# Neighbouring PSUM banks for pairs, with re-searched product tables, in a two-layer matmul kernel

## The chip, the cores and the metric

The kernel runs on one core of one Trainium2 chip. The metric is the device time of one launch in microseconds (us). The kernel before took 941.87 us (median of 3 runs, 941.43 to 942.97).

## The reference

```python
y = np.matmul(x, w1) + b1        # x (16, 512, 768), w1 (768, 3072)
y = np.maximum(y, 0)
return np.matmul(y, w2)          # w2 (3072, 768), all float32
```

In flat form, 8192 rows of x go through a first product (768 to 3072), bias and relu, and a second product (3072 to 768).

## The kernel before, in words

**Fewer products.** Both products are done by a recursive scheme of the Strassen kind in float16. Tables at the top of the file describe it. A first product of 3 x 2 blocks takes 20 block products instead of 24 (`FIRST_U`, `FIRST_V`), on sums of x blocks (`X_SUMS`) and of w1 blocks (`W1_SUMS`); a second product likewise takes 20 (`SECOND_U`, `SECOND_V`, `Y_SUMS`, `W2_SUMS`). `FIRST_OPS` and `SECOND_OPS` list what is done with the finished products in PSUM: write an output ('out'), keep a sum in SBUF ('sum'), or put the value in the PSUM of another chain as its start ('seed'). `FIRST_CHAINS` and `SECOND_CHAINS` say which products (m) and operations (t) follow each other in one piece of PSUM, and `FIRST_ORDER` and `SECOND_ORDER` give the order in which TensorE takes the products.

**Iterations.** There are 16, numbered 0 to 15: 8 blocks of 1024 rows for the first half of the hidden width, then 8 for the second half. Iteration 0 computes its first product plainly, without the scheme (L821). Each other iteration has two stages on TensorE: 40 first products of 6 matmuls each (L911, 256 columns), and 20 second products of 8 matmuls each (L1032, 384 columns). During the first stage ScalarE (ACT) and VectorE (DVE) evict into y (L941, L945, L948, L951, L957). During the second stage they work on pairs of banks (L1044 on ACT, L1047 on DVE), DVE adds y blocks (L884) and x blocks of the next iteration (L661), SyncE (SP) issues transposing DMAs into x (L612), and stores go out from SP or, with accumulation in DRAM, from GpSimd (POOL) (L1075, L1077). In the last iteration POOL adds sums to earlier results (L1085).

**PSUM.** The tile `ps` has 8 banks of 512 float32 on 128 partitions. A first product fills one bank. A second product needs two banks, for rows j = 0 and j = 1, and the eviction of both is one instruction over a view with the stride between the two banks. That view is `pair` (L1022 to L1024):

```python
        def pair(reg):
            a, b = reg.at
            return self.ps[:, a:b + 1:b - a, 0:NH]
```

**The order of the work.** Class `Graph` is a planner. Each piece of work is added with an engine and a written-in duration; `run` places the pieces in time on the five queues, and in `take` (L297 to L318) picks the banks for each piece of PSUM, by when they come free. In before, a pair is any two banks that come free first. The instructions are then issued in the planned order, each engine working strictly through its own queue. Semaphore waits are not written by hand: the layer that records the instructions adds them, from the regions of the tiles that each one reads and writes.

**Fused sums.** Two sums that follow each other in `X_SUMS` or `Y_SUMS` can be done by one DVE instruction over a strided view; `X_FUSE` and `Y_FUSE` name where.

Of the kernel before, what the change touches and what calls it, by code (L numbers as in the profile page):

```python
# [27 lines left out]

X_SUMS = ((20, 7, 5, -1), (18, 3, 2, -1), (13, 0, 6, -1), (8, 4, 5, -1), (22, 6, 7, -1), (21, 7,
    1, -1), (23, 4, 6, -1), (11, 2, 5, -1), (10, 3, 1, -1), (19, 4, 2, -1), (15, 2, 1, -1), (9, 6,
    5, -1), (12, 2, 0, -1), (17, 6, 1, -1), (16, 1, 0, -1), (14, 3, 5, -1))
FIRST_U = (8, 9, 21, 18, 2, 13, 20, 19, 1, 14, 10, 17, 11, 22, 6, 12, 5, 23, 15, 16)
W1_SUMS = ((6, 2, 5, 1), (8, 6, 4, -1), (17, 1, 8, -1), (7, 0, 1, 1), (10, 8, 7, -1), (16, 3, 10,
    -1), (9, 6, 3, -1), (11, 5, 4, -1), (12, 9, 0, -1), (14, 7, 9, -1), (15, 3, 5, -1), (13, 7, 2,
    -1))
FIRST_V = (2, 9, 4, 11, 17, 1, 3, 1, 16, 4, 3, 14, 8, 15, 12, 0, 6, 0, 10, 13)
FIRST_OPS = {
    0: (2, 1, 15, 1, 'out', 0, None),  # L40
    1: (3, 1, None, None, 'out', 1, (1.0, 1.0, -1.0)),
    2: (3, 1, 15, 1, 'out', 2, None),
    3: (0, 1, None, None, 'out', 3, None),
    4: (7, 1, 17, 1, 'out', 4, None),
    5: (7, 1, 19, 1, 'out', 5, None),
    6: (5, 1, 18, 1, 'out', 6, None),
    7: (4, 1, 17, 1, 'out', 7, None),
    8: (1, 1, 19, 1, 'out', 8, None),
    9: (6, 1, 18, 1, 'out', 9, None),
    10: (2, 1, None, None, 'out', 10, (0.0, 1.0, 0.0)),  # L50
    11: (6, 1, None, None, 'out', 11, (0.0, 0.0, 1.0)),
    12: (7, 1, None, None, 'seed', 4, None),
    13: (2, 1, None, None, 'seed', 3, (-1.0, 0.0, 1.0)),
    14: (6, 1, None, None, 'seed', 5, None),
    15: (8, -1, None, None, 'sum', None, (1.0, 0.0, 0.0)),
    16: (8, -1, 20, 1, 'seed', 0, None),
    17: (8, 1, 19, 1, 'sum', None, (0.0, 1.0, -1.0)),
    18: (2, -1, 20, 1, 'sum', None, None),
    19: (6, 1, None, None, 'sum', None, (0.0, 0.0, 1.0)),
    20: (2, 1, None, None, 'sum', None, (1.0, 0.0, 0.0)),  # L60
}
FIRST_CHAINS = ((('m', 10), ('t', 3)), (('m', 0), ('t', 8)), (('m', 8), ('t', 20), ('t', 0), ('m',
# [4 lines left out]
FIRST_SEEDS = (16, None, None, 13, 12, 14, None, None, None)  # L67
FIRST_ORDER = (36, 4, 16, 20, 12, 0, 8, 7, 9, 18, 24, 28, 10, 1, 15, 3, 21, 38, 32, 14, 35, 29,
    27, 30, 11, 34, 23, 26, 37, 31, 6, 5, 17, 25, 2, 22, 13, 33, 39, 19)
SWITCH_ORDER = (36, 4, 16, 20, 12, 0, 8, 7, 9, 18, 24, 28, 10, 1, 15, 3, 21, 38, 32, 14, 35, 29,  # L70
    27, 30, 11, 34, 23, 26, 37, 31, 6, 5, 17, 25, 2, 22, 13, 33, 39, 19)

Y_SUMS = ((16, 3, 0, 1), (21, 5, 3, 1), (15, 8, 7, 1), (12, 11, 10, 1), (19, 5, 16, 1), (18, 1,
    15, 1), (20, 2, 19, 1), (14, 6, 9, -1), (17, 11, 14, -1), (22, 1, 17, 1), (26, 18, 20, 1),
    (24, 7, 22, 1), (13, 4, 12, -1), (23, 11, 9, 1), (27, 13, 14, 1), (25, 13, 16, -1))
SECOND_U = (6, 2, 8, 26, 5, 21, 17, 23, 27, 19, 13, 4, 25, 12, 15, 11, 24, 18, 0, 1)
W2_SUMS = ((9, 2, 0, -1), (11, 9, 5, -1), (7, 2, 1, -1), (15, 5, 7, -1), (6, 5, 4, 1), (8, 6, 3,
    -1), (14, 8, 9, -1), (13, 3, 11, 1), (10, 7, 8, -1), (16, 10, 0, -1), (12, 7, 6, -1), (17, 5,
    2, -1))
SECOND_V = (0, 5, 7, 17, 9, 0, 10, 3, 16, 11, 14, 1, 13, 4, 1, 8, 12, 15, 3, 4)  # L80
W2_NEG = (4,)
SECOND_OPS = {
    0: (0, 1, 11, 1, 'out', 4, None),
    1: (2, 1, 9, 1, 'out', 5, None),
    2: (1, 1, 11, 1, 'out', 6, None),
    3: (2, 1, None, None, 'out', 7, None),
    4: (1, 1, 8, 1, 'out', 2, None),
    5: (3, -1, 8, 1, 'out', 3, None),
    6: (0, -1, 9, 1, 'out', 0, None),
    7: (3, 1, None, None, 'out', 1, None),  # L90
    8: (1, -1, 13, 1, 'sum', None, None),
    9: (0, 1, 10, 1, 'sum', None, None),
    10: (4, 1, 16, -1, 'sum', None, None),
    11: (5, 1, None, None, 'sum', None, None),
    12: (5, -1, None, None, 'seed', 0, None),
    13: (6, 1, None, None, 'sum', None, None),
    14: (5, 1, 16, 1, 'seed', 2, None),
    15: (1, -1, None, None, 'seed', 5, None),
    16: (1, 1, None, None, 'sum', None, None),
    17: (3, -1, 19, 1, 'seed', 1, None),  # L100
    18: (4, -1, None, None, 'seed', 3, None),
    19: (6, 1, None, None, 'sum', None, None),
# [6 lines left out]
SECOND_SEEDS = (12, 17, 14, 18, None, 15, None)  # L109
SECOND_ORDER = (19, 5, 1, 4, 9, 17, 13, 18, 15, 10, 12, 6, 7, 11, 2, 0, 14, 8, 16, 3)  # L110
LAST_ORDER = (19, 5, 1, 4, 9, 17, 13, 18, 15, 10, 12, 6, 7, 11, 2, 0, 14, 8, 16, 3)

X_FUSE = (3, 8, 11)
Y_FUSE = (2, 13)


def general_path(ctx, tc, xf, w1, b1, w2, of):
# [113 lines left out]
class Graph:  # L231
# [57 lines left out]
    def held(self, reg, at):  # L289
# [3 lines left out]
            self.places[reg.kind][i][0] = 1e9  # L293
        return reg

    def take(self, reg, start):

        p = self.places[reg.kind]
        if reg.kind == "ps":
            if reg.seeded:  # L300
                found = sorted((max(f, start), -full, i) for i, (f, full) in enumerate(p)
                               if full >= (2 if reg.seeded == 2 else 1))
            else:
                found = sorted((max(f, start), full, i) for i, (f, full) in enumerate(p))
            if len(found) < reg.n or found[reg.n - 1][0] > 1e8:
                return None
            at = sorted(i for _, _, i in found[:reg.n])
            return found[reg.n - 1][0], at
        best = None
        step = reg.n if reg.kind == "s" else 1  # L310
        for i in range(0, len(p) - reg.n + 1, step):
            f = max(p[k][0] for k in range(i, i + reg.n))
            if f < 1e8 and (best is None or f < best[0]):
                best = (f, list(range(i, i + reg.n)))
        return best
# [134 lines left out]
class Fast:  # L450
# [442 lines left out]
    def add_first(self, it):  # L893
# [12 lines left out]
        def product(p, ch, start):  # L906
            at = bank[ch].at[0]
            gi, p = divmod(p, np)
            for j in range(2):
                for k in range(3):  # L910
                    nc.tensor.matmul(  # L911
                        self.ps[:, at, j * self.QM:(j + 1) * self.QM],
                        lhsT=self.v1[:, gi, self.w1s[FIRST_V[p]], k, j * P:(j + 1) * P],
                        rhs=self.x[:, self.xs[FIRST_U[p]], k, :],
                        start=(start and j == 0 and k == 0), stop=(k == 2),
# [46 lines left out]
        for kind, n in sequence(chains, seeds, ops, SWITCH_ORDER if switch else FIRST_ORDER):  # L962
            if kind == "m":
# [46 lines left out]
    def add_second(self, it):  # L1010
# [7 lines left out]
        NH, QM = self.NH, self.QM  # L1018
# [1 line left out]
        last = [n for k, n in steps if k == "t" and SECOND_OPS[n][4] == "out"][-1]  # L1020

        def pair(reg):  # L1022
            a, b = reg.at
            return self.ps[:, a:b + 1:b - a, 0:NH]  # L1024

        def product(p, ch, start):
            sj = [(s, j) for s in range(4) for j in range(2)]
# [61 lines left out]
        for kind, n in steps:  # L1089
            if kind == "m":  # L1090
                ch = where[n]
                start = ch not in bank
# [8 lines left out]
            ch, a, u, b, what, to, _ = SECOND_OPS[n]  # L1101
# [231 lines left out]
```

## Time and profile before

| what | value |
|---|---|
| median of 3 runs | 941.87 us |
| the profiled execution | 942.75 us, span 941.1 us |
| granted TensorE clock, mean | 0.998 |
| busy over the span: PE, DVE, ACT, POOL | 865.2, 690.3, 477.8, 142.9 us |
| DMA queues, share of 16 engines | 42.0% (software), 25.5% (hardware) |

The profile is of one execution. Its page gives busy time by engine, the chain of work that ended last, and groups of equal instructions. "PE" is the matmul part of TensorE; "idle before" is the time the engine stood still just ahead of an instruction, with the instruction that released it. The busy time of PE counts overlapping matmuls once, so what it leaves of the span is idle time. The profile names tiles but not banks; the banks of an instruction and the semaphore counts that it waits for stand in the built program.

### The profile page before, as it was taken

The page shows a single profiled execution, that of the slowest core. Times are in us where ns is not written, and L with a number is a line of the kernel's source. Part 1 is how long each engine was busy: PE and PEld are TensorE (multiplying, and loading weights), DVE is VectorE, ACT ScalarE, POOL GpSimd, SP SyncE. Part 2 cuts the span into 40 slices and gives each one's busy share as a digit, 9 for nine tenths or more (in the row PEclk, how much of TensorE's full clock was granted, in tenths as well). Part 3 has the DMA queues.
Part 4 walks back from the last instruction along what each step waited for, and adds up shares of the span by engine and source line. Part 5 has one row for each costly group of instructions (what it writes and reads, how often), then busy time and mean ns, then how long its engine had stood idle before and what let it go on. Part 6 is the DMA issues. An engine that isn't in the chain of part 4 may idle for free.

```text
span 941.1 us, 16251 instructions
## 1 busy us (share of the span) xinstructions
PE 865.2 (92%) x6445; PEld 631.1 (67%) x6445; DVE 690.3 (73%) x1052; ACT 477.8 (51%) x951; POOL 142.9 (15%) x155
## 2 busy tenths in 40 slices
PE   8998989799897988989989999999989999899996
PEld 7567558486584855848668685866848576585763
DVE  3788768667686676776889879676867868668673
ACT  6866647366473662633745253744728325253340
POOL 5113100101001010000030402213030130401204
PEclk9999999999999999999999999999999999999999
DMA  9999583836638347361697958688686677943743
GB/s 211 193 220 194 95 198 68 159 101 87 175 68 160 99 77 185 69 134 68 223 200 115 134 85 133 112 116 128 102 116 104 103 117 102 144 75 51 104 133 135
DMA packets 162979, 119.86 MB, mean 127 GB/s; under 512 B 93244, under 2 KB 161364, under 8 KB 162644
## 3 DMA queue, kind: packets, MB, share of 16 engines
q0 software_dynamic: 49760, 58.99, 42.0%
q1 hardware_dynamic: 112672, 58.81, 25.5%
q8 instruction: 51, 0.84, 0.4%
q10 hardware_dynamic: 468, 1.00, 0.3%
q14 instruction: 28, 0.23, 0.1%
HBM read 73.94 MB, written 59.77 MB: 142 GB/s over the span
## 4 chain that ended last, share of the span: by engine, by line
PE 73%; DVE 10%; DMA 6%; issue 4%; ACT 4%; POOL 1%; SPq 0%; DVEq 0%; POOLq 0%; ACTq 0%
PE ps L911 39%; PE ps L1032 31%; DVE o L1047 3%; PE ps L821 3%; DVE y L884 3%; DMA x<-xn 2%; DVE s L1047 2%; DMA out_dram<-o 2%; ACT ps L1044 2%; DVE x L661 1%; DMA out_dram<-s 1%; ACT o L1044 1%; DMA v<-in_w_dram 1%; ACT xn L620 1%; DVE ps L1047 1%
## 5 line engine op out<-in xcount | busy, mean ns | idle before, releaser
L1032 PE MATMUL ps<-v,y 128*128 128x384 f16 x2560 | 430.9, 326 | 56.6 <-ACT ps L1044 18.9
L911 PE MATMUL ps<-x,v 128*128 128x256 f16 x3600 | 398.6, 273 | 9.4 <-DVE o L1047 2.6
L1032 PEld LDWEIGHTS <-y 128*128 128x128 f16 x2560 | 249.7, 98 | 233.6 <-issue 74.1
L911 PEld LDWEIGHTS <-v 128*128 128x128 f16 x3600 | 352.5, 98 | 54.6 <-issue 10.1
L948 DVE CUSTOM_DVE_ANT_0 y<-ps,s 128x512 f16<-128x512 f32 x240 | 157.6, 687 | 79.2 <-PE ps L911 75.3
L884 DVE TENSOR_TENSOR y<-y 128x1024 f16<-128x1024 f16 (+2 forms) x242 | 170.2, 718 | 8.5 <-ACT y L830 5.2
L945 ACT ACTIVATE s<-ps,bt 128x256 f32<-128x256 f32 x180 | 75.3, 469 | 141.1 <-PE ps L911 122.0
L661 DVE TENSOR_TENSOR x<-x 128x768 f16<-128x768 f16 (+1 forms) x182 | 112.8, 644 | 15.3 <-DMA x<-xn 14.3
L1077 POOL DMA_DIRECT2D out_dram<-o x68 | 81.6, 1282 | 213.9 <-DMA out_dram<-s 74.3
L1044 ACT ACTIVATE ps<-ps 128x768 f32<-128x768 f32 x48 | 38.2, 795 | 147.3 <-PE ps L1032 105.9
L558 POOL DMA_DIRECT2D xn<-in_x_dram x30 | 22.7, 758 | 523.9 <-ACT xn L620 334.7
L1044 ACT ACTIVATE s<-ps 128x768 f32<-128x768 f32 x64 | 51.8, 810 | 78.5 <-PE ps L1032 77.9
L1047 DVE TENSOR_TENSOR o<-ps,s 128x768 f32<-128x768 f32 x52 | 48.9, 955 | 51.4 <-PE ps L1032 46.9
L945 ACT ACTIVATE y<-ps,bt 128x256 f16<-128x256 f32 x180 | 70.3, 482 | 13.4 <-PE ps L911 13.4
L620 ACT ACTIVATE xn<-xn 128x768 f16<-128x768 f16 x60 | 50.1, 838 | 3.8 <-DMA x<-xn 3.6
L941 ACT ACTIVATE ps<-ps 128x512 f32<-128x512 f32 x60 | 34.8, 580 | 24.6 <-PE ps L911 17.4
L1044 ACT ACTIVATE o<-ps 128x768 f32<-128x768 f32 x42 | 33.7, 808 | 11.2 <-PE ps L1032 6.4
L1047 DVE TENSOR_TENSOR s<-ps,s 128x768 f32<-128x768 f32 x32 | 30.5, 953 | 8.0 <-PE ps L1032 8.0
L945 ACT ACTIVATE ps<-ps,bt 128x256 f32<-128x256 f32 x60 | 26.8, 447 | 14.1 <-PE ps L911 10.9
L821 PE MATMUL ps<-x,v 128*128 128x256 f16 (+1 forms) x216 | 32.1, 308 | 0.9 <-DMA v<-in_w_dram 0.6
L1047 DVE TENSOR_TENSOR o<-s,ps 128x768 f32<-128x768 f32 x26 | 24.6, 948 | 6.4 <-DMA out_dram<-o 2.3
L1047 DVE TENSOR_TENSOR ps<-ps,s 128x768 f32<-128x768 f32 x16 | 15.5, 966 | 18.8 <-ACT o L1044 10.5
(63 smaller groups left out, 366.7 us busy)
## 6 DMA issues: line engine op xcount, KB each, us to landing
out_dram<-o POOLq DMA_DIRECT2D x68, 384.0 KB, 6.3
out_dram<-o SPq DMA_DIRECT2D x59, 384.0 KB, 3.4
xn<-in_x_dram POOLq DMA_DIRECT2D x28, 768.0 KB, 7.5
out_dram<-s SPq DMA_DIRECT2D x12, 384.0 KB, 5.8
x<-out_dram SPq DMA_DIRECT2D x8, 384.0 KB, 4.0
v<-in_w_dram POOLq DMA_DIRECT2D x6, 384.0 KB, 9.0
v<-in_w_dram POOLq DMA_DIRECT2D x12, 192.0 KB, 10.3
w1d<-in_w_dram POOLq DMA_DIRECT2D x6, 384.0 KB, 11.0
```

Of the source, the lines that this page charges most:

```text
L620: self.nc.scalar.activation(out=self.xn[:, s, :], in_=self.xn[:, s, :], func=ACTF.Square, accum_out=self.stat[:, self.stat_at["x"] + i:][: ...
L661: self.nc.vector.tensor_tensor(out=self.two(x, out), in0=self.two(x, in0), in1=self.two(x, in1), op=ALU.add if sign > 0 else ALU.subtract)
L821: nc.tensor.matmul(self.ps[:, ps.at[0], cols], lhsT=self.v1[:, gi, 2 * h + k2, k, j * P:(j + 1) * P], rhs=rhs, start=(k2 == 0 and k == 0), ...
L884: self.nc.vector.tensor_tensor(out=self.two(y, out), in0=self.two(y, in0), in1=self.two(y, in1), op=ALU.add if sign > 0 else ALU.subtract)
L911: nc.tensor.matmul(self.ps[:, at, j * self.QM:(j + 1) * self.QM], lhsT=self.v1[:, gi, self.w1s[FIRST_V[p]], k, j * P:(j + 1) * P], rhs=sel ...
L941: nc.scalar.activation(out=out, in_=ps, scale=float(a), func=func if kind == "out" else ACTF.Copy)
L945: nc.scalar.activation(out=out[:, halves[j]], in_=ps[:, halves[j]], func=func, scale=float(a), bias=beta(j))
L948: nc.vector._custom_dve(TENSOR_ADD_SAT, out=out, in0=ps, in1=s, s0=F_MAX, s1=0.0)
L1032: nc.tensor.matmul(self.ps[:, bank[ch].at[j], 0:NH], lhsT=self.y[:, self.ys[SECOND_U[p]], m0:m0 + P], rhs=self.v2[:, slot[SECOND_V[p]], s, :],
L1044: nc.scalar.activation(out=out, in_=ps, func=ACTF.Copy, scale=float(a))
L1047: engine.tensor_tensor(out=out, in0=in0, in1=in1, op=ALU.add if a == b else ALU.subtract)
L1077: nc.gpsimd.dma_start(out=rows, in_=out, accum_op=ALU.add)
```

## The change

Four things are changed.

1. In `take`, a pair is always two neighbouring banks, 0-1, 2-3, 4-5 or 6-7, and `pair` is a plain slice.
2. In `take`, a single bank is picked by the time that it comes free as before, but among equals first one whose neighbour is not free (`spare`).
3. The tables at the top are replaced by others that compute the same function: the sums of x and y, most sums of w2, the places of the first products, the chains of the first product, and the orders. `SECOND_CHAINS` and `SECOND_SEEDS` stay, `W1_SUMS` changes in the order of two operands. The numbers of products, and of operations of each kind, stay.
4. `X_FUSE` goes from 3 to 4 places and `Y_FUSE` from 2 to 3, so each iteration has one DVE instruction fewer of each kind.

```diff
+    def spare(self, i, start):
+        return self.places["ps"][i ^ 1][0] <= start
...
             if reg.seeded:
-                found = sorted((max(f, start), -full, i) for i, (f, full) in enumerate(p)
+                found = sorted((max(f, start), self.spare(i, start), -full, i)
+                               for i, (f, full) in enumerate(p)
                                if full >= (2 if reg.seeded == 2 else 1))
             else:
-                found = sorted((max(f, start), full, i) for i, (f, full) in enumerate(p))
-            if len(found) < reg.n or found[reg.n - 1][0] > 1e8:
+                found = sorted((max(f, start), self.spare(i, start), full, i)
+                               for i, (f, full) in enumerate(p))
+            if reg.n == 2:
+                at = {i: f for f, _, _, i in found}
+                found = sorted((max(f, at[i + 1]), i) for i, f in at.items()
+                               if i % 2 == 0 and i + 1 in at)
+                if not found or found[0][0] > 1e8:
+                    return None
+                f, i = found[0]
+                return f, [i, i + 1]
+            if not found or found[0][0] > 1e8:
                 return None
-            at = sorted(i for _, _, i in found[:reg.n])
-            return found[reg.n - 1][0], at
+            return found[0][0], [found[0][3]]
...
-SECOND_ORDER = (19, 5, 1, 4, 9, 17, 13, 18, 15, 10, 12, 6, 7, 11, 2, 0, 14, 8, 16, 3)
+SECOND_ORDER = (19, 5, 1, 4, 9, 18, 13, 17, 10, 15, 12, 11, 6, 7, 2, 0, 14, 8, 16, 3)
...
-X_FUSE = (3, 8, 11)
-Y_FUSE = (2, 13)
+X_FUSE = (6, 8, 10, 12)
+Y_FUSE = (5, 10, 13)
...
         def pair(reg):
-            a, b = reg.at
-            return self.ps[:, a:b + 1:b - a, 0:NH]
+            a = reg.at[0]
+            return self.ps[:, a:a + 2, 0:NH]
```

In the built programs DVE's TensorTensor instructions go from 731 to 702; ACT's activations (830), DVE's evictions of L948 (240), the matmuls and the DMAs stay the same in number.

More of the change, by code (lines that the diff above doesn't have):

```diff
@@ L25 @@
 X_LO, W1_LO, W2_LO = 1.0, 1.0, 0.5
[L31 to L34, printed above, removed]
+X_SUMS = ((20, 4, 3, -1), (15, 4, 1, -1), (21, 7, 1, -1), (12, 0, 4, -1), (10, 5, 1, -1), (13, 0,
+    6, -1), (11, 2, 6, -1), (22, 6, 7, -1), (16, 0, 1, -1), (17, 6, 1, -1), (23, 6, 3, -1), (14,
+    7, 3, -1), (18, 3, 2, -1), (19, 4, 2, -1), (9, 4, 5, -1), (8, 5, 3, -1))
@@ L35 @@
+FIRST_U = (22, 13, 17, 8, 16, 19, 6, 14, 1, 4, 21, 18, 10, 3, 11, 9, 12, 20, 23, 15)
 W1_SUMS = ((6, 2, 5, 1), (8, 6, 4, -1), (17, 1, 8, -1), (7, 0, 1, 1), (10, 8, 7, -1), (16, 3, 10,
-    -1), (9, 6, 3, -1), (11, 5, 4, -1), (12, 9, 0, -1), (14, 7, 9, -1), (15, 3, 5, -1), (13, 7, 2,
+    -1), (9, 6, 3, -1), (11, 4, 5, -1), (12, 9, 0, -1), (14, 7, 9, -1), (15, 3, 5, -1), (13, 7, 2,
     -1))
-FIRST_V = (2, 9, 4, 11, 17, 1, 3, 1, 16, 4, 3, 14, 8, 15, 12, 0, 6, 0, 10, 13)
+FIRST_V = (15, 0, 9, 3, 2, 0, 12, 4, 6, 17, 3, 13, 4, 16, 1, 11, 1, 10, 14, 8)
@@ L39 @@
 FIRST_OPS = {
[L40 to L51, printed above, removed]
@@ L52 @@
-    12: (7, 1, None, None, 'seed', 4, None),
-    13: (2, 1, None, None, 'seed', 3, (-1.0, 0.0, 1.0)),
-    14: (6, 1, None, None, 'seed', 5, None),
+    0: (0, 1, 18, 1, 'out', 0, None),
+    1: (4, 1, 17, 1, 'out', 1, None),
+    2: (3, 1, 19, 1, 'out', 2, None),
+    3: (6, 1, 15, 1, 'out', 3, None),
+    4: (7, 1, None, None, 'out', 4, (1.0, 1.0, -1.0)),
+    5: (7, 1, 15, 1, 'out', 5, None),
+    6: (2, 1, None, None, 'out', 6, None),
+    7: (5, 1, 17, 1, 'out', 7, None),
+    8: (5, 1, 19, 1, 'out', 8, None),
@@ L55 @@
+    9: (1, 1, 18, 1, 'out', 9, None),
+    10: (6, 1, None, None, 'out', 10, (0.0, 1.0, 0.0)),
+    11: (1, 1, None, None, 'out', 11, (0.0, 0.0, 1.0)),
+    12: (0, 1, None, None, 'seed', 1, None),
+    13: (6, 1, None, None, 'seed', 7, (-1.0, 0.0, 1.0)),
+    14: (4, 1, None, None, 'seed', 5, None),
     15: (8, -1, None, None, 'sum', None, (1.0, 0.0, 0.0)),
-    16: (8, -1, 20, 1, 'seed', 0, None),
+    16: (8, -1, 20, 1, 'seed', 2, None),
     17: (8, 1, 19, 1, 'sum', None, (0.0, 1.0, -1.0)),
-    18: (2, -1, 20, 1, 'sum', None, None),
@@ L59 @@
-    19: (6, 1, None, None, 'sum', None, (0.0, 0.0, 1.0)),
-    20: (2, 1, None, None, 'sum', None, (1.0, 0.0, 0.0)),
-}
-FIRST_CHAINS = ((('m', 10), ('t', 3)), (('m', 0), ('t', 8)), (('m', 8), ('t', 20), ('t', 0), ('m',
[4 rows of a table removed]
[L67 to L79, printed above, removed]
@@ L80 @@
-SECOND_V = (0, 5, 7, 17, 9, 0, 10, 3, 16, 11, 14, 1, 13, 4, 1, 8, 12, 15, 3, 4)
-W2_NEG = (4,)
-SECOND_OPS = {
[L83 to L90, printed above, removed]
+    18: (6, -1, 20, 1, 'sum', None, None),
+    19: (0, 1, None, None, 'sum', None, (0.0, 0.0, 1.0)),
@@ new lines @@
+    20: (6, 1, None, None, 'sum', None, (1.0, 0.0, 0.0)),
+}
+FIRST_CHAINS = ((('m', 8), ('t', 19), ('m', 2), ('t', 12), ('m', 1), ('t', 0)), (('m', 10), ('t',
[4 rows of a table added]
+FIRST_SEEDS = (None, 12, 16, None, None, 14, None, 13, None)
+FIRST_ORDER = (19, 8, 9, 24, 28, 13, 17, 4, 22, 29, 12, 3, 16, 5, 15, 33, 39, 37, 6, 32, 25, 36,
+    23, 2, 18, 30, 26, 14, 1, 38, 35, 7, 10, 34, 21, 20, 27, 11, 0, 31)
+SWITCH_ORDER = (19, 8, 9, 24, 28, 13, 17, 4, 22, 29, 12, 3, 16, 5, 15, 33, 39, 37, 6, 32, 25, 36,
+    23, 2, 18, 30, 26, 14, 1, 38, 35, 7, 10, 34, 21, 20, 27, 11, 0, 31)
@@ new lines @@
+Y_SUMS = ((13, 8, 7, 1), (16, 5, 3, 1), (12, 2, 1, 1), (20, 7, 10, 1), (15, 4, 12, -1), (24, 2, 0,
+    1), (19, 10, 13, 1), (23, 15, 9, -1), (26, 23, 3, -1), (14, 0, 6, -1), (17, 2, 14, 1), (18, 9,
+    16, 1), (27, 14, 15, -1), (22, 17, 20, 1), (21, 18, 19, 1), (25, 11, 21, 1))
+SECOND_U = (4, 11, 5, 25, 8, 13, 15, 12, 27, 19, 17, 6, 22, 24, 16, 2, 26, 18, 10, 9)
+W2_SUMS = ((7, 2, 1, -1), (13, 7, 5, -1), (6, 2, 0, -1), (10, 5, 6, -1), (8, 5, 4, -1), (9, 3, 8,
+    1), (12, 7, 9, -1), (15, 8, 7, -1), (11, 9, 6, -1), (14, 1, 11, 1), (16, 3, 10, 1), (17, 5, 2,
+    -1))
@@ L91 @@
+SECOND_V = (1, 5, 6, 17, 7, 1, 11, 4, 14, 13, 12, 0, 15, 3, 0, 9, 16, 10, 4, 3)
+W2_NEG = (3,)
+SECOND_OPS = {
+    0: (0, 1, 11, 1, 'out', 2, None),
+    1: (2, 1, 9, 1, 'out', 3, None),
+    2: (1, 1, 11, 1, 'out', 0, None),
+    3: (2, 1, None, None, 'out', 1, None),
+    4: (1, 1, 8, 1, 'out', 4, None),
+    5: (3, -1, 8, 1, 'out', 5, None),
+    6: (0, -1, 9, 1, 'out', 6, None),
+    7: (3, 1, None, None, 'out', 7, None),
     8: (1, -1, 13, 1, 'sum', None, None),
     9: (0, 1, 10, 1, 'sum', None, None),
-    10: (4, 1, 16, -1, 'sum', None, None),
+    10: (4, 1, 16, 1, 'sum', None, None),
@@ L96 @@
     13: (6, 1, None, None, 'sum', None, None),
-    14: (5, 1, 16, 1, 'seed', 2, None),
+    14: (5, 1, 16, -1, 'seed', 2, None),
     15: (1, -1, None, None, 'seed', 5, None),
-    16: (1, 1, None, None, 'sum', None, None),
+    16: (1, -1, None, None, 'sum', None, None),
     17: (3, -1, 19, 1, 'seed', 1, None),
@@ L109 @@
 SECOND_SEEDS = (12, 17, 14, 18, None, 15, None)
-SECOND_ORDER = (19, 5, 1, 4, 9, 17, 13, 18, 15, 10, 12, 6, 7, 11, 2, 0, 14, 8, 16, 3)
-LAST_ORDER = (19, 5, 1, 4, 9, 17, 13, 18, 15, 10, 12, 6, 7, 11, 2, 0, 14, 8, 16, 3)
-X_FUSE = (3, 8, 11)
-Y_FUSE = (2, 13)
+SECOND_ORDER = (19, 5, 1, 4, 9, 18, 13, 17, 10, 15, 12, 11, 6, 7, 2, 0, 14, 8, 16, 3)
+LAST_ORDER = (19, 5, 1, 4, 9, 18, 13, 17, 10, 15, 12, 11, 6, 7, 2, 0, 14, 8, 16, 3)
+X_FUSE = (6, 8, 10, 12)
+Y_FUSE = (5, 10, 13)
 def general_path(ctx, tc, xf, w1, b1, w2, of):
```

8 rows, old and new, of the table FIRST_CHAINS are left out of this document.

## The prediction

> **What bounds the kernel now.** First the page: who is busy.
>
> ```profile
> span 941.1 us, 16251 instructions
> PE 865.2 (92%) x6445; PEld 631.1 (67%) x6445; DVE 690.3 (73%) x1052; ACT 477.8 (51%) x951; POOL 142.9 (15%) x155
> L1032 PE MATMUL ps<-v,y 128*128 128x384 f16 x2560 | 430.9, 326 | 56.6 <-ACT ps L1044 18.9
> L911 PE MATMUL ps<-x,v 128*128 128x256 f16 x3600 | 398.6, 273 | 9.4 <-DVE o L1047 2.6
> ```
>
> PE is the bound, and of its 76 us of idle time 56.6 lie before matmuls of the second product. Then the waits of PE: whom it waited for.
>
> ```profile
> PE ps L1032 <- ACT ps L1044: 18.9, 23, 1.5
> PE ps L1032 <- DVE o L1047: 15.6, 16, 2.0
> PE ps L1032 <- DVE s L1047: 15.2, 16, 1.2
> ```
>
> The stalls are many and short, about 1 us each, behind operations on pairs of banks. Then busy time by stretch, cut where L911 and L1032 begin: the first stage of iteration 3 and its second stage, the second stage of iteration 8, that of iteration 10 (columns: length, then PE, PEld, DVE, ACT, POOL).
>
> ```profile
> 191.18:217.41 26.23, 26.23 (x242) 23.45 (x241) 19.94 (x33) 20.64 (x47) 0.00 (x0) 1.00 0.37 86
> 217.41:249.97 32.56, 27.12 (x162) 15.60 (x160) 22.01 (x30) 12.53 (x22) 3.54 (x5) 1.00 0.76 145
> 510.31:536.63 26.32, 26.31 (x162) 15.63 (x160) 24.72 (x35) 7.78 (x11) 7.96 (x7) 1.00 0.94 136
> 617.91:648.51 30.60, 26.64 (x162) 15.62 (x160) 23.17 (x32) 8.32 (x12) 7.78 (x8) 1.00 0.91 124
> ```
>
> The same 160 matmuls take 26.3 us in iteration 8, without a gap, and 29.7 to 33.6 in the twelve iterations 1 to 6 and 10 to 15. So a first stage is worth 26.2 us, a second 26.3, and what lies above is stall. Last the timeline of PE in iteration 3, one line per run without a gap:
>
> ```profile
> 217.41 9.27 PE L1032 MATMUL ps<-v,y 128*128 128x384 f16 x56
> 227.37 1.46 PE L1032 MATMUL ps<-v,y 128*128 128x384 f16 x8 [0.70 <-DVE s L1047]
> 229.77 5.76 PE L1032 MATMUL ps<-v,y 128*128 128x384 f16 x33 [0.94 <-ACT ps L1044]
> 236.45 1.30 PE L1032 MATMUL ps<-v,y 128*128 128x384 f16 x7 [0.92 <-DVE o L1047]
> 238.63 4.06 PE L1032 MATMUL ps<-v,y 128*128 128x384 f16 x24 [0.88 <-ACT ps L1044]
> 243.84 2.92 PE L1032 MATMUL ps<-v,y 128*128 128x384 f16 x17 [1.15 <-DVE s L1047]
> 247.54 2.60 PE L1032 MATMUL ps<-v,y 128*128 128x384 f16 x15 [0.78 <-DVE o L1047]
> ```
>
> **What these waits are for.** The built program gives each instruction's banks and awaited counts; laid beside the trace they say which instruction PE awaited. At 227.37 PE writes bank 3 and awaits a DVE operation that reads banks 2 and 4. At 238.63 it writes bank 5 and awaits an ACT operation from banks 0 and 1 to banks 3 and 6. At 229.77 it writes bank 0, which it must await, but that ACT operation (from 5 and 7 to 0 and 1) had itself waited for the product in banks 3 and 6. All follow one pattern: a strided view over banks a and b is taken as everything from a to b. In the whole program before, 84 of PE's waits, 51 of ACT's and 75 of DVE's are for an instruction that shares no bank and nothing in SBUF, only such a stretch. Call these enclosed waits. In the changed program I count none, as a neighbouring pair encloses nothing.
>
> Next I measured every gap of PE: start minus the start before, minus a matmul's pace (109.2 ns for 256 columns, 163.2 for 384, the steps inside the runs above). From each gap I followed what ended last: the awaited instruction, what had held that, and so on. 67 gaps with 66.9 us end at an enclosed wait: 39.4 us directly (47 gaps), 27.5 through an operation held by one. By iteration these are 6.0 to 6.6 us in 1 to 6, 1.3 or less in 7 to 9, 4.6 to 5.4 in 10 to 12, 2.5 to 4.3 in 13 to 15, with 1.1 at L1160.
>
> **The change part by part.**
> *Neighbouring pairs, the gain.* All 66.9 us go, if no true wait is late in their place. One exception: in the last iteration POOL's additions (L1085, three of 1.81 us, back to back from 929.5 to 934.9) hold the end, so the 2.13 us stall at 933.77 brings nothing. Counted: -66.9 + 2.1 = -64.8. Time per access does not enter: by distance 1 to 5 between the two banks, L1044 takes 795 to 810 ns and L1047 950 to 966.
> The Trainium skill (PSUM — Partial Sum Buffer, "PSUM bank collisions raise a hardware error") has engines kept apart on the same bank and lets them run together on different banks. By this rule every enclosed wait is needless; the constant durations agree.
>
> *Neighbouring pairs, the cost.* There are now 4 pairs, not 28, so a pair may come free later. I read the new order for it. In iterations 5 and 10 of the changed program no matmul awaits an operation whose own product lies less than one product back: 1.31 us in the second stage, two first products (1.31) in the first. Before, iterations 10 to 12 had waits with nothing between. A pair operation needs 0.20 us (matmul end to start) + 0.81 (ACT) or 0.955 (DVE) + 0.05 = 1.06 or 1.21, so it fits by 0.1 us if its engine is free. ACT is (12.5 us busy of 32.6). DVE is not quite, so I laid its queue end to end: L948 at 0.69, y sums 0.69 or fused 1.22, x sums 0.55 or 0.95. In iteration 5 (clock from its first matmul), the last L948 runs 26.41 to 27.10, four y sums end at 30.39, the seed awaited by product 4 ends at 31.35 against 31.43. Five y sums and two x sums end at 37.4; the sums and seed for products 11 and 12 end at 39.3 and 40.4 against 40.57 and 41.88. The sum for product 16 ends at 47.0 against 47.10. The last outputs end 1.4 us before their banks are needed by the next first stage. So two places fit by under 0.1 us. I take 0.1 us an iteration, +1.5 over 15; bounds 0 and 0.4 (one x sum's 0.55 less the margin), so 0 to +6.
>
> *First-product tables.* The same matmuls, evictions and DMAs in another order; before, this stage ran at 26.2 us unstalled in ten iterations. An L948 or L957 at 0.69 + 0.25 = 0.94 us against 1.31 fits: 0. The start (4.7 us of waits on loads and DVE in iteration 1's first stage) is reordered too: bounds -2 and +4, taken 0.
>
> *x sums moved.* Before, three x sums awaiting transposes stood in DVE's queue ahead of the last L948: where the transposes were late (iterations 5, 6, 9, 13), PE lost 3.55 us in 7 gaps. In the new order they stand behind the seed and five y sums, 8 us after the last transposes may start (two issues of 1.28 us, landing 2.8 median, 8.2 at worst). Taken -2.0; bounds -3.55 and, if transposes come late by what they cost in iteration 6 (1.03) in each of 14 iterations, +14.4. Queued behind such an x sum is a sum that products 11 and 12 need.
>
> *Fusing.* 29 DVE instructions fewer: 14 x (2 x 0.55 - 0.95) + 15 x (2 x 0.687 - 1.217) = 4.5 us of DVE, beside PE: 0; with no cover it is the margin of 0.1 us above.
>
> *Clock.* After the check ahead of iteration 14 PE runs 16 matmuls at 212 ns, not 109: 1.6 us.
>
> ```profile
> 820.00:826.00 6.00, 5.03 (x32) 3.81 (x32) 2.11 (x4) 2.05 (x5) 1.44 (x2) 0.72 1.11 161
> ```
>
> 0.72 is the clock. Stalls of 1.3 us elsewhere cost no clock. The check remains: 0.
> The Trainium skill (TensorE: Matmul & The Clock Gate, "What's actually happening") has the clock halved after a window of about 3.4 us with PE idle. Two stalls of 1.1 us and the check lie here; the rule would let the shorter idle keep the clock, and the sum would be 1.6 lower.
>
> **Sum.** 942.75 - 64.8 + 1.5 - 2.0 = 877.4 for the profiled execution, which is 0.9 above the median of the runs; so 876.5.
>
> **Rivals.**
> - *DVE or DMA takes over.* An iteration shrinks from 57-60 us to 52.6, DVE's 42 us in it (the two stretches above) then fill 80%, and the queues' 67% become 72%. For: margins under 0.1 us, late transposes in 4 iterations. Against: iteration 8's second stage kept pace with DMA at 0.94. Price: +14.4 and +1.5 on 877: 893. Chance 0.19 (885 to 898).
> - *Only the direct part goes.* Where an operation was late through an enclosed wait, another true wait stands just as late: 942.75 - 39.4 - 0.9 = 902.5. For: few pairs. Against: the distances above. Chance 0.08.
> - *Slower: pairs run short.* Second products have seven waits per iteration at just one product's distance, 105 in all. If DVE or ACT fell behind there by a pair operation each (0.81 us), the loss is 85 against a gain of 64.8: 962. It decides at 0.62 us per wait. Against: the queue laid out above. Chance 0.03.
> - *It doesn't do what it says*, some wait remains as wide: 942. The program shows none left: 0.02.
>
> **Forecast** 876.5, chance 0.68 (868 to 885). Low end: the rest of the late transposes (-1.6), no lateness at products 4 and 16 (-1.5), the clock (-1.6), the end (-2.1), the start (-2): 868. High end: the first rival's price, 893. Together these hold about 0.8. This kernel can be told from no change by about 0.2%. Faster 0.95, same 0.02, slower 0.03.
>
> **What would show it.** PE's idle before L1032 falls from 56.6 to under 10, and second stages to 26.3 to 27 us in every iteration; busy times of PE, ACT and POOL stay; DVE's falls by 4 to 5. If pairs run short, waits of PE on ACT or DVE at L1032's successor stay near 1 us each. If DMA takes over, x sums idle for transposes and L948 or the y sums come late. I am wrong if the enclosed waits hid true ones, or if the layer adds waits that I did not find by banks.

## The result and the profile after

The kernel after took 877.32 us (median of 4 runs, 875.98 to 879.5) against 941.73 us before (4 runs, 941.43 to 942.97): ratio 0.9316, 95% interval 0.9295 to 0.9337. The forecast was 876.5. The profiled execution took 876.98 us.

All lines of the file shift by 13: L911 is now L924, L1032 is L1045, ACT's L1044 is L1057, DVE's L1047 is L1060. From the page of after, who is busy, and the two groups of matmuls:

```profile
span 875.3 us, 16234 instructions
PE 855.2 (98%) x6445; PEld 635.0 (73%) x6445; DVE 686.8 (78%) x1023; ACT 478.9 (55%) x951; POOL 143.2 (16%) x155
...
L1045 PE MATMUL ps<-v,y 128*128 128x384 f16 x2560 | 419.3, 326 | 1.1 <-DVE o L1060 0.6
L924 PE MATMUL ps<-x,v 128*128 128x256 f16 x3600 | 398.5, 273 | 10.0 <-ACT ps L958 6.1
```

Idle time before second products falls from 56.6 to 1.1 us. That before first products goes from 9.4 to 10.0 us, but it is another one, as the waits of PE show:

```profile
PE ps L924 <- ACT ps L958: 6.1, 1, 6.1
PE ps L924 <- ACT o L1057: 2.8, 2, 1.9
PE ps L1045 <- DVE o L1060: 0.6, 1, 0.6
```

Where 55 waits of about 1 us stood, there is now one of 6.1 us in a first stage. Busy time by stretch, with the columns as before: the second stages of iterations 3, 8 and 10, then the first stage of iteration 1, then 5 us inside that stage:

```profile
213.28:239.34 26.06, 26.06 (x162) 15.65 (x160) 23.77 (x31) 14.03 (x26) 3.54 (x5) 1.00 0.80 154
474.91:500.91 26.00, 26.00 (x163) 15.65 (x160) 23.78 (x34) 7.63 (x11) 7.82 (x7) 1.00 0.91 137
579.34:605.34 26.00, 26.00 (x163) 15.66 (x161) 23.68 (x32) 9.30 (x14) 7.23 (x7) 1.00 0.86 132
70.28:108.88 38.60, 29.00 (x242) 24.34 (x240) 22.72 (x36) 22.54 (x50) 7.29 (x7) 0.91 0.99 163
102.00:107.00 5.00, 4.59 (x25) 3.32 (x25) 1.80 (x3) 3.28 (x9) 0.00 (x0) 0.57 0.34 69
```

Iteration 3's second stage took 32.56 us before, and its timeline had seven runs of matmuls. Now it is one run:

```profile
213.28 26.23 PE L1045 MATMUL ps<-v,y 128*128 128x384 f16 x160
```

The same holds in iterations 0 to 14: 26.0 to 26.3 us. So the stage is bounded by its matmuls alone. Measured by stages, the 65.8 us of the span came and went here:

| stretch | change, us |
|---|---|
| start to the first second-product matmul | +1.3 |
| second stage of iteration 0 | -0.5 |
| first stage of iteration 1 (30.9 to 38.6) | +7.7 |
| second stages of iterations 1 to 14 (429.9 to 364.9) | -65.0 |
| first stages of iterations 2 to 15 | -6.3 |
| last iteration's second stage and end (37.04 to 34.03) | -3.0 |

The +1.3 lies in PE's 24 identity matmuls at the start (L763 before, L776 after), which took 418 ns each instead of 275; here are the two groups, before and after:

```profile
L763 PE MATMUL ps<-ident,o 128*128 128x128 f32 x24 | 3.0, 275 | 0.8 <-DMA o<-in_x_dram 0.6 <-DVE x L771 0.3
L776 PE MATMUL ps<-ident,o 128*128 128x128 f32 x24 | 5.3, 418 | 0.6 <-DMA o<-in_x_dram 0.6
```

In the trace of before the full clock begins 5.1 us after the start, in that of after only at 10.7 us. This seems to go with the run, not with the change: the stretch ended at 44.0 us in e12 (396 ns) and at 43.8 in e8 (385 ns), and between 42.6 and 43.1 us in the other runs (275 to 330 ns). The +7.7 is the new stall. Timelines of ACT, then of PE, around it:

```profile
91.77 0.57 ACT L954 ACTIVATE ps<-ps 128x512 f32<-128x512 f32 x1
99.88 0.84 ACT L633 ACTIVATE xn<-xn 128x768 f16<-128x768 f16 x1 [7.54 <-DMA x<-xn]
...
100.72 0.82 ACT L958 ACTIVATE y<-ps,bt 128x256 f16<-128x256 f32 x2
```

```profile
102.41 6.63 PE L924 MATMUL ps<-x,v 128*128 128x256 f16 x42 [6.08 <-ACT ps L958]
```

A square of xn (L633, whose result no matmul of this stage awaits) overwrites xn, so it must wait for the transposing DMAs that read it. Those were late, and the square stood in ACT's queue ahead of evictions L958 that PE needed. PE lost 6.1 us, and then ran 17 matmuls at 0.21 us instead of 0.109: the stretch 102 to 107 shows a granted clock of 0.57. That is about 1.8 us more.

### The profile page after: what moved, and what is told of

It reads as the page before. It is cut to its first block, busy times and chain, and to the rows that moved or that the text cites. A ratio compares the mean times of both kernels' runs of the same rounds, so it can differ in the third digit from the quotient of the medians.

```text
span 875.3 us, 16234 instructions
## 1 busy us (share of the span) xinstructions
PE 855.2 (98%) x6445; PEld 635.0 (73%) x6445; DVE 686.8 (78%) x1023; ACT 478.9 (55%) x951; POOL 143.2 (16%) x155
## 3 DMA queue, kind: packets, MB, share of 16 engines
q1 hardware_dynamic: 112672, 58.81, 27.5%
## 4 chain that ended last, share of the span: by engine, by line
PE 88%; DMA 4%; issue 4%; DVE 1%; POOL 1%; ACT 1%; SPq 0%; POOLq 0%; DVEq 0%; ACTq 0%
PE ps L924 42%; PE ps L1045 42%; PE ps L834 4%; DMA out_dram<-o 1%; DMA x<-xn 1%; POOL x L1098 1%; DMA out_dram<-s 1%; DVE v L690 1%; PE ps L776 1%; DMA o<-in_x_dram 1%; DVE s L1060 0%; DMA x<-out_dram 0%; ACT s L958 0%; DVE ps L1060 0%; ACT junk L728 0%
## 5 line engine op out<-in xcount | busy, mean ns | idle before, releaser
L1045 PE MATMUL ps<-v,y 128*128 128x384 f16 x2560 | 419.3, 326 | 1.1 <-DVE o L1060 0.6
L924 PE MATMUL ps<-x,v 128*128 128x256 f16 x3600 | 398.5, 273 | 10.0 <-ACT ps L958 6.1
L924 PEld LDWEIGHTS <-v 128*128 128x128 f16 x3600 | 353.1, 98 | 54.4 <-issue 11.1
L1045 PEld LDWEIGHTS <-y 128*128 128x128 f16 x2560 | 250.4, 98 | 165.8 <-issue 2.0
L961 DVE CUSTOM_DVE_ANT_0 y<-ps,s 128x512 f16<-128x512 f32 x240 | 161.4, 688 | 72.7 <-PE ps L924 53.7
L897 DVE TENSOR_TENSOR y<-y 128x1024 f16<-128x1024 f16 (+2 forms) x227 | 165.6, 755 | 8.7 <-ACT y L843 6.2
L958 ACT ACTIVATE s<-ps,bt 128x256 f32<-128x256 f32 x180 | 73.8, 472 | 109.9 <-PE ps L924 106.6
L674 DVE TENSOR_TENSOR x<-x 128x768 f16<-128x768 f16 (+1 forms) x168 | 109.5, 684 | 0.5
L1057 ACT ACTIVATE ps<-ps 128x768 f32<-128x768 f32 x48 | 38.2, 795 | 108.9 <-PE ps L1045 90.4
L1057 ACT ACTIVATE s<-ps 128x768 f32<-128x768 f32 x64 | 51.7, 809 | 61.9 <-PE ps L1045 61.3
L958 ACT ACTIVATE y<-ps,bt 128x256 f16<-128x256 f32 x180 | 73.6, 471 | 20.2 <-PE ps L924 18.4
L633 ACT ACTIVATE xn<-xn 128x768 f16<-128x768 f16 x60 | 50.2, 838 | 9.5 <-DMA x<-xn 9.3
L1060 DVE TENSOR_TENSOR o<-ps,s 128x768 f32<-128x768 f32 x52 | 49.1, 954 | 7.5 <-PE ps L1045 4.1
L1057 ACT ACTIVATE o<-ps 128x768 f32<-128x768 f32 x42 | 33.9, 808 | 21.5 <-PE ps L1045 13.5
L1060 DVE TENSOR_TENSOR s<-ps,s 128x768 f32<-128x768 f32 x32 | 30.6, 956 | 14.3 <-PE ps L1045 13.7
L970 DVE TENSOR_TENSOR s<-s,ps 128x512 f32<-128x512 f32 x30 | 20.5, 684 | 20.1 <-PE ps L924 20.1
L958 ACT ACTIVATE ps<-ps,bt 128x256 f32<-128x256 f32 x60 | 26.9, 448 | 17.1 <-PE ps L924 8.1
L954 ACT ACTIVATE ps<-ps 128x512 f32<-128x512 f32 x60 | 35.0, 584 | 0.7
L1060 DVE TENSOR_TENSOR o<-s,ps 128x768 f32<-128x768 f32 x26 | 24.7, 950 | 7.8 <-DMA out_dram<-o 6.8
```

The source lines that it names most:

```text
L633: self.nc.scalar.activation(out=self.xn[:, s, :], in_=self.xn[:, s, :], func=ACTF.Square, accum_out=self.stat[:, self.stat_at["x"] + i:][: ...
L674: self.nc.vector.tensor_tensor(out=self.two(x, out), in0=self.two(x, in0), in1=self.two(x, in1), op=ALU.add if sign > 0 else ALU.subtract)
L897: self.nc.vector.tensor_tensor(out=self.two(y, out), in0=self.two(y, in0), in1=self.two(y, in1), op=ALU.add if sign > 0 else ALU.subtract)
L924: nc.tensor.matmul(self.ps[:, at, j * self.QM:(j + 1) * self.QM], lhsT=self.v1[:, gi, self.w1s[FIRST_V[p]], k, j * P:(j + 1) * P], rhs=sel ...
L954: nc.scalar.activation(out=out, in_=ps, scale=float(a), func=func if kind == "out" else ACTF.Copy)
L958: nc.scalar.activation(out=out[:, halves[j]], in_=ps[:, halves[j]], func=func, scale=float(a), bias=beta(j))
```

## The experiments

The theory: a two-bank view with a stride is recorded as all banks from the first to the second, so instructions wait for others that share no bank with them ("enclosed waits"); neighbours end that. Rivals: the new tables (orders, chains, sums) bring the gain; far banks cost time by themselves; or the fused sums bring it. The kernel before took 941.2 to 943.8 us beside these runs.

**e1, the banks alone: the kernel before with the new choice of banks.** The edit is the `take` and `pair` part of the diff shown above, on the old tables.

> The tables, orders and fusing of before; only the choice of banks (neighbouring pairs, and singles that leave pairs whole) and the plain slice are those of after. The built program has no enclosed wait (before: 84 of PE, 51 of ACT, 75 of DVE). Theory (enclosed waits cost the 65 us): 876 to 892; the upper end if the old order, not searched for this rule, has some true waits. Rival (the re-searched tables and orders bring the gain): 925 or more. Rival (only the 39 us of direct stalls were the banks', the rest the order's): about 902.

Measured: 906.62 us (906.16 to 907.53), ratio 0.9623 [0.9598, 0.9649]. Outside what the theory expected. Its groups:

```profile
L1045 PE MATMUL ps<-v,y 128*128 128x384 f16 x2560 | 420.5, 326 | 4.0 <-ACT ps L1057 2.8 <-DVE y L961 0.6 <-DVE o L1060 0.6
L924 PE MATMUL ps<-x,v 128*128 128x256 f16 x3600 | 405.2, 275 | 30.7 <-DVE ps L970 15.1 <-ACT ps L954 11.0 <-ACT o L1057 2.3
...
L942 PE MATMUL ps<-ident 128*128 128x128 f16 x9 | 2.0, 219 | 0.0
```

Most second stages are as after the change (26.0 us): that part of the theory holds. But the first stages lose 21 us, behind seeds (L954, L970). One of them, PE's timeline in iteration 3:

```profile
248.29 3.44 PE L924 MATMUL ps<-x,v 128*128 128x256 f16 x30 [1.42 <-ACT ps L954]
251.56 0.22 PE L942 MATMUL ps<-ident 128*128 128x128 f16 x1
252.64 15.55 PE L924 MATMUL ps<-x,v 128*128 128x256 f16 x141 [0.86 <-DVE ps L970]
```

L942 is a filler matmul that the kernel before did not have: the planner found no bank wholly written before, took one whose tail was not and filled it. Seven first stages lost 2.3 us each so (1.42 and 0.86), that of iteration 1 lost 3.1 us behind L970, and the one at the switch of halves 6.0 us. Which of the two rules of the new `take` does this, e9 tells.

**e2, the tables alone: the kernel after with the old choice of banks and the strided view.** The edit is the reverse of e1's.

> The other half alone: the tables, orders and fusing of after, with the bank choice of before (any two banks, strided view). The built program has 52 enclosed waits of PE, 68 of ACT and 55 of DVE. Theory: the stalls come back in proportion to PE's enclosed waits, 65 x 52/84 = 40 us above 877, so 905 to 930. Rival (tables bring the gain): 885 or less.

Measured: 951.5 us (951.23 to 952.81), ratio 1.010 [1.0074, 1.0127]: 1.0% slower than before, which nothing I wrote allowed for. The tables bring nothing as long as the stride stays. Of the 10 us, 7.3 lie in iteration 1's first stage, which takes 38.2 us, about as long as in after. The waits of PE have the old form:

```profile
PE ps L1032 <- ACT ps L1044: 20.9, 25, 1.2
PE ps L1032 <- DVE o L1047: 15.7, 16, 1.0
PE ps L1032 <- DVE ps L1047: 10.4, 10, 1.1
```

PE has fewer enclosed waits than before (52 for 84), yet 70 gaps with 77.3 us end at one. My price per wait was wrong: what counts is how much work of PE stands between the awaited instruction's product and the waiting one. In second stages, PE's waits with no work of PE between number 56 here, 25 in the kernel before.

**e3, no stride in the kernel before: each pair operation split into two, one per bank.** Plan, order and banks stay.

```diff
         def pair(reg):
-            a, b = reg.at
-            return self.ps[:, a:b + 1:b - a, 0:NH]
+            return [self.ps[:, i, 0:NH] for i in reg.at]
...
-                combine(nc.scalar if alone else nc.vector, out, ps, a,
-                        None if alone else sum_of(kept[u]), b)
+                for j in range(2):
+                    combine(nc.scalar if alone else nc.vector, half(out, j), half(ps, j), a,
+                            None if alone else sum_of(kept[u])[:, j], b)
```

> Before with its own plan and its own banks, at distances 1 to 5; each operation on a pair is done as two instructions, one per bank, so no view is strided and the built program has no enclosed wait. DVE gets 165 instructions more, ACT 154; a pair takes about 2 x 0.55 us on DVE for 0.955. Theory: most of the stalls go, but a pair operation at one product's distance no longer fits (0.20 + 1.10 + 0.05 = 1.35 us against 1.31): 880 to 905. Rival (far pairs are slow or run short by themselves, whatever the view): 940 or more.

Measured: 873.62 us (871.85 to 874.5), ratio 0.9278 [0.9252, 0.9303]: the whole gain, with old tables, old banks and old order, and faster than the 880 to 905 that I expected. A group, and the second stage of iteration 3:

```profile
L1034 PE MATMUL ps<-v,y 128*128 128x384 f16 x2560 | 420.2, 326 | 1.8 <-DVE y L948 0.8 <-ACT ps L1046 0.7
```

```profile
204.07:230.07 26.00, 26.00 (x163) 15.65 (x160) 23.67 (x41) 13.07 (x31) 3.55 (x5) 1.00 0.80 157
```

I had expected a charge for the added instructions: a pair takes DVE 2 x 0.55 us instead of 0.955, ACT 2 x 0.49 instead of 0.81. DVE's busy time indeed rises to 700.1 us, but PE hardly waits for it (0.8 us before second products): in the program, a product's first matmul now awaits only the half that frees its own bank.

**e4, stride back under the new plan.** The kernel after, with its banks renamed once planned, so that each pair lies four banks apart.

```diff
         self.g.run(begin=5.0)
+        banks = (0, 4, 1, 5, 2, 6, 3, 7)
+        for reg in {r for t in self.g.tasks for r in t.regs if r.kind == "ps"}:
+            reg.at = [banks[i] for i in reg.at]
...
         def pair(reg):
-            a = reg.at[0]
-            return self.ps[:, a:a + 2, 0:NH]
+            a, b = reg.at
+            return self.ps[:, a:b + 1:b - a, 0:NH]
```

> After with its plan and order unchanged, but each pair's two banks renamed from 2k and 2k+1 to k and k+4, so that the view has a stride of 4 banks. The built program has 198 enclosed waits of PE, 223 of ACT, 191 of DVE. Theory: slower than before: 65 x 198/84 = 153 us above 877 if each costs what it cost before; 960 to 1060. Rival (the tables and the order bring the gain, or the far banks cost nothing): 877 to 885.

Measured: 1182.06 us (1180.36 to 1183.04), ratio 1.2543 [1.2508, 1.2578]. The direction was as expected, the size was not: 305 us more than after. The group of second products, and the second stage of iteration 3:

```profile
L1045 PE MATMUL ps<-v,y 128*128 128x384 f16 x2560 | 468.0, 327 | 247.7 <-DVE o L1060 51.7 <-ACT s L1057 49.5 <-DVE s L1060 45.8
```

```profile
259.25:303.35 44.10, 28.88 (x163) 15.52 (x161) 22.95 (x29) 14.24 (x26) 3.54 (x5) 1.00 0.52 105
```

ACT and DVE are busy for as long as in after (14.24 and 22.95 against 14.03 and 23.77 us), one pair operation takes what it took (L1057 795 to 810 ns, L1060 952 to 966), and PE stands still for 15 of 44 us. The program has 198 enclosed waits of PE, 223 of ACT and 191 of DVE, and 282 waits in second stages have under 1.3 us of PE's work between.

**e5 and e6, split under the new plan, near banks and far ones.** The kernels after and e4, each with the split of e3.

> After (neighbouring pairs, its own plan), with each pair operation done as two instructions, one per bank. No enclosed wait either way, so this prices the splitting by itself: 165 DVE and 154 ACT instructions more, about 0.15 us more per pair operation on DVE. Theory: nothing to gain, 0 to 12 us to lose, since DVE's queue had under 0.1 us to spare at two places: 877 to 889. If splitting gained much by itself (a product's first matmul awaits only its own bank's half), the reading of the run that split the kernel before would have to be taken back: 866 or less would say so.

> The renamed far banks (k and k+4) of the run at 1182 us, with each pair operation split by bank: same banks, same plan, no strided view, no enclosed wait. Theory: the whole loss of 305 us goes, and the time is that of after with the same split, within 3 us. Rival (far banks are slow by themselves): stays above 1000.

Measured: e5 874.3 us (873.76 to 875.31), ratio 0.9280 [0.9265, 0.9296]; e6 874.39 us (873.46 to 876.06), ratio 0.9284 [0.9265, 0.9303]. Without a stride all of e4's loss is gone, and banks four apart cost what neighbours cost. So the loss is the view's, not the banks'. And with no enclosed wait to remove, splitting is worth 3 us at most, so shorter pieces alone do not explain e3. That e5's median is 3 us below that of after was not expected, and where these 3 us lie stays open: the profiled spans differ by 1.5 us (873.8 and 875.3), of which 1.2 lie in the slow matmuls at the start, and iteration 1's first stage is no shorter (39.4 and 38.6).

**e7, the second rule taken out of the kernel after.**

```diff
     def spare(self, i, start):
-        return self.places["ps"][i ^ 1][0] <= start
+        return False
```

> After without the rule that single banks leave pairs whole (spare is always false); pairs stay neighbours. The order was searched with the rule. Built program: the distances of PE's waits stay nearly as they are (one wait at 0.8 us of PE work more). Theory: 876 to 880, the rule is worth little with this order. Rival (the rule is what makes pairs come free): 885 to 905.

Measured: 877.18 us (876.1 to 879.26), ratio 0.9316 [0.9296, 0.9337], as expected: with the new tables, single banks that leave pairs whole bring nothing.

**e9, the same edit in e1.**

> The run at 906.6 us (old tables, neighbouring pairs) without the rule for single banks. In that run PE stood 2.5 us in each of 8 first stages at two first products whose bank was the source of a seed with no product in between (18 waits of PE at no distance, 3 in before), and 6 us at the switch to the second half. Without the rule 2 such waits are left. Theory (with the old order it is the single-bank rule, not the neighbouring pairs, that keeps 29 us of the gain back): 906.6 - 20 to 28 = 878 to 887. Rival (the pairs themselves run short): 900 to 907.

Measured: 880.89 us (878.65 to 880.95), ratio 0.9344 [0.9326, 0.9363], as expected. The filler matmuls are gone (6445 matmuls, as before) and waits of PE at no distance in the first stages fall from 18 to 2. So neighbouring pairs alone bring 61 of 64 us on the old tables; the rule for single banks cost e1 its 26 us there, and the new tables are what makes that rule harmless. Beside after (877.3) the new tables are thus worth 3.6 us net: in after, first stages 2 to 15 take 367.5 us, in e9 374.8, but iteration 1's first stage takes 38.6 us for 31.6.

**e10, new tables with any banks, split.** The kernel e2 with the split of e3.

> The run at 951.5 us (new tables, any two banks, strided) with each pair operation split by bank, so that nothing is strided and the built program has no enclosed wait. Theory: all of its loss goes and it stands with the other split versions, 872 to 878: once no wait is enclosed, neighbouring or far, free or bound choice of banks make no difference of over 5 us. Rival (pairs must be neighbours or the order does not fit): 890 or more.

Measured: 874.09 us (873.41 to 876.78), ratio 0.9283 [0.9249, 0.9317], as expected. Beside e2 (951.5) it shows again that the stride alone is what costs, under any plan tried.

**e8, no fused sums.** The kernel after with:

```diff
-X_FUSE = (6, 8, 10, 12)
-Y_FUSE = (5, 10, 13)
+X_FUSE = ()
+Y_FUSE = ()
```

> After with X_FUSE and Y_FUSE empty: 101 DVE instructions more, 14 x 4 x 0.15 + 15 x 3 x 0.16 = 15.6 us more of DVE over all, 1.1 us an iteration, in the y sums and x sums ahead of the places that fitted by under 0.1 us in the prediction. The planner knows the costs and may reorder. Theory (DVE has 10 us to spare per iteration, only its few tight places count): 878 to 890. Rival (DVE is hidden throughout): 876 to 878. Rival (DVE is the bound now): 877 + 15 = 892 or more.

Measured: 873.0 us (870.19 to 873.94), ratio 0.9256 [0.9222, 0.929]: faster, which neither expectation had. DVE has 803 TensorTensor instructions instead of 702 and is busy 695.3 us, and the second stages stay at 26.0 to 26.3. The gain is elsewhere: the planner placed the start otherwise, the stall behind L958 in iteration 1's first stage was 2.6 us instead of 6.1, and the stage took 35.0 instead of 38.6 us. Fusing is hidden; of the margins of under 0.1 us that I had laid out nothing was seen, perhaps because the planner reorders the sums when their number changes; that was not tested. As a measure of fusing this run is spoiled by the start.

**e11, the new stall taken away.** The planner is told that the transposes for iteration 2 and the stores of iteration 0 land later, so it queues the squares behind the evictions.

```diff
-                out=self.x_part(s), in_=self.xn[:, s, :]), lat=1.6, reads=[("xn", s)],
+                out=self.x_part(s), in_=self.xn[:, s, :]), lat=8.0 if it == 2 else 1.6,
+                reads=[("xn", s)],
...
-                           writes=[("out", self.block(it), to)], lat=6.5)
+                           writes=[("out", self.block(it), to)], lat=6.5 if it else 10.0)
```

> After with two durations in the planner changed: transposes of iteration 2 land after 8 us in the plan, not 1.6, and stores of iteration 0 after 10, not 6.5. In after's first stage of iteration 1 ACT stands 7.5 us before a square (L633) that awaits transposes, PE then 6.2 us behind ACT, and runs 17 matmuls at half the clock (1.7 us). In the new plan these squares stand behind the evictions. Theory: 877.3 - 7.9 = 869, or 867 if the waits for stores (5 us) shrink too. Rival (the DMA queues are full there, another wait takes its place): 874 to 878.

Measured: 868.33 us (867.4 to 868.84), ratio 0.9211 [0.9182, 0.9241], as expected. Iteration 1's first stage takes 30.2 us instead of 38.6. The 6.1 us wait is gone from the waits of PE, and the longest is now this one:

```profile
PE ps L925 <- ACT o L1058: 2.4, 1, 2.4
```

Which of the two latencies does it was not separated.

**e12, e5 and e11 together.**

> Both changes that seem to help: after with pair operations split by bank (874.3 us) and the two planner durations of the run on late squares. In the split run PE stood 4.1 us behind the square and 4.1 behind a store in iteration 1, with about 3 us at half the clock. Theory: 865 to 870, faster than before, after and the split runs. Rival (start bound by DMA): 873 to 876.

Measured: 867.32 us (866.52 to 869.8), ratio 0.9212 [0.918, 0.9245]; not told apart from e11. Both beat both kernels. In e12's page PE is busy 99% of the span:

```profile
PE 852.4 (99%) x6445; PEld 633.8 (73%) x6445; DVE 696.4 (81%) x1188; ACT 489.8 (57%) x1105; POOL 143.3 (17%) x155
```

## Why the prediction was right, and where not

**The cause: right, and shown.** It was argued from banks and semaphore counts. The runs part it from the rivals named: no stride on old banks gives the whole gain (e3), a stride under the new plan takes it away (e4), the split gives it back on the same far banks (e6), and new tables without neighbours bring nothing (e2). The constant durations of pair operations, which the prediction took as a sign, show only that distance costs nothing. That PE may go on while others use other banks shows in e6: the banks and the plan are those of e4, no such wait is left, each half operation takes 0.47 to 0.56 us, and 308 us are gone.

**The size of the main term: right.** -64.8 was counted from gaps that end at an enclosed wait, not from the number of such waits. No enclosed wait stands in the program after, so no gap ends at one. The 65.0 us that second stages 1 to 14 gave look like the same number but are another sum: they hold the 3.55 us of late x sums, less 0.6 us of new waits, so about 62 us of enclosed waits; the rest of those lay in first stages and in the last iteration. The same gap-by-gap way gave 77.3 us in e2, where the number of waits would have said less than before. The rival "only the direct part goes" (902.5) fell: the indirect 27.5 us went as well.

**Pairs short, and products 4 and 16.** I took +1.5 with bounds 0 and +6. Measured 0.6: product 16 of iteration 4 waited 0.33 us, that of iteration 7 0.24. That place was named rightly, and nearly always it fits; product 4 never waited so. DVE at 78% did not take over, so the rivals at 893 and 962 fell.

**x sums moved.** Taken -2.0; the 3.55 us of late transposes went whole. The move also shows in the chain of work that ended last, where DVE has 1% for 10% before (this also holds the enclosed waits):

```profile
PE 88%; DMA 4%; issue 4%; DVE 1%; POOL 1%; ACT 1%; SPq 0%; POOLq 0%; DVEq 0%; ACTq 0%
```

**The start: wrong.** The step "bounds -2 and +4, taken 0" failed: +7.7 in iteration 1's first stage. I had looked at what PE awaits in that stage before, not at what the new plan put on ACT's queue ahead of the evictions: a square that awaits a DMA. e11 takes 8.4 us off that stage, so it is the cause. It came with the new tables, not with the banks: in every run with new tables but e4 this stage took 35.0 us or more until e11 changed the plan, and in e3 and e9, with old ones, 30.6 and 31.6. The late transposes, which I had weighed for x sums on DVE, struck on ACT.

**The clock: wrong.** I took 0 and left the -1.6 as the other case. It came. In the 5 us behind the kernel's own check ahead of iteration 14 the clock is now full:

```profile
763.00:768.00 5.00, 4.57 (x42) 3.98 (x41) 2.52 (x4) 2.41 (x6) 2.40 (x2) 1.00 1.14 163
```

Before, PE's timeline had two stalls around the check, of 0.98 and 1.02 us, with eight matmuls between them; now one of 0.43 us is left, and no matmul is slowed. The Trainium skill (TensorE: Matmul & The Clock Gate, "What's actually happening") has the clock halved after an idle window of about 3.4 us. By this rule the shorter idle keeps the clock, and so it was; but by it the two stalls before, 2.0 us in all, should have kept it too, and there the granted clock was 0.50 from 821 to 824 us. The last section shows how much idle was enough.

**The end.** I counted -1.1 for the last iteration (its enclosed waits less what POOL holds); -3.0 came. Two waits there shrank, from 2.13 to 0.73 us and from 1.66 to 0.42; POOL's additions held less than I thought.

**Fusing: 0, right**, by DVE's 3.5 us less that show nowhere (4.5 by count); e8, spoiled as a measure by its start, does not speak against it.

So the total is within 0.8 us partly because errors cancel: the first stage of iteration 1 cost 7.7 and the slower matmuls at the start 1.3 more than taken, against some 9 us that were not counted or counted low (the end, the clock, tight places, x sums, first stages).

## What to carry to other kernels

Before an engine is blamed for many short waits, ask of each what it is for: if waiter and awaited share no memory, the region that was recorded is too wide, and a plain slice over neighbours or one instruction per piece removes it (941 to 874 us here, with nothing else changed). Price such waits by following each gap to what ended last in it; their number says little (52 waits cost 77 us, 84 cost 67). In an engine that works strictly in order, look for low-priority work that awaits a DMA ahead of work that the bound engine needs.

## What the hardware showed

- The clock fell to half after much less idle time than I had thought, and the length of one stall does not decide it. A stall of 6.1 us did it in after and one of 6.0 us in e1, but so did one of 2.36 us in e11 and two stalls of 1 us with eight matmuls between in the kernel before. Stalls of 1.91 us (after) and 2.04 us (e12) did not, and of two equal ones in e8 that of 2.62 us did not and that of 2.63 us did. From e11, by stretch (68 to 71, to 73.4, to 75, to 76, to 77, to 78 us), the granted clock is the third column from the end:

```profile
68.00:71.00 3.00, 3.00 (x23) 2.07 (x22) 2.93 (x6) 0.35 (x2) 0.68 (x1) 1.00 1.12 255
71.00:73.40 2.40, 0.04 (x2) 0.03 (x1) 2.40 (x4) 2.35 (x5) 0.00 (x0) 0.93 1.14 260
73.40:75.00 1.60, 1.60 (x8) 1.13 (x8) 1.41 (x3) 1.44 (x3) 0.00 (x0) 0.50 1.11 250
75.00:76.00 1.00, 1.00 (x7) 0.72 (x5) 1.00 (x3) 0.00 (x0) 0.00 (x0) 0.50 1.12 260
76.00:77.00 1.00, 1.00 (x9) 0.79 (x8) 0.67 (x1) 0.33 (x1) 0.00 (x0) 0.77 1.07 393
77.00:78.00 1.00, 1.00 (x11) 0.90 (x10) 0.00 (x0) 1.00 (x3) 0.00 (x0) 1.00 0.93 344
```

  What decides shows when the time is cut on a grid. From the first change to the last, each trace holds its full and its half clock for whole multiples of 3.413 us. Cut so, e8's two stalls fall into windows in which PE was busy for 1.46 and for 1.13 us; below, each of these windows and the next one (the second number is PE's busy time, the third from the end the clock):

```profile
71.13:74.54 3.41, 1.46 (x14) 1.16 (x12) 1.76 (x3) 0.19 (x1) 0.00 (x0) 1.00 1.13 262
74.54:77.95 3.41, 2.12 (x18) 1.76 (x18) 1.74 (x3) 2.00 (x4) 1.18 (x1) 1.00 1.01 190
95.02:98.44 3.42, 1.13 (x11) 0.87 (x9) 1.84 (x3) 2.16 (x6) 0.00 (x0) 1.00 0.98 205
98.44:101.85 3.41, 3.07 (x15) 2.15 (x15) 0.32 (x1) 2.65 (x7) 0.00 (x0) 0.50 0.30 58
```

  Up to the last matmul of each of the 14 traces, all 14 windows of full clock with PE busy for at most 1.38 us were followed by half clock, and none with 1.50 us or more; in between, half of eight were. So a stall costs clock when it leaves PE about 1.4 us or less in one such window (roughly, as the ends of matmuls are modelled), and where the grid lies differs from run to run. The half clock lasted 3.4 or 6.8 us; outside e4 it cost 1.2 to 2.9 us each time.

- The time of a pair operation does not depend on how far its banks lie apart (1 to 5), and splitting it costs DVE 15% (1.10 for 0.955 us) and ACT 21% (0.98 for 0.81); neither showed in the time.
